# Two-layer hybrid decoder trunk: the up projection as three 256-column matmuls a weight tile, and its activation made for two tiles at once

## Chip, cores and metric

The kernel runs on one core of a Trainium2 chip. The metric is the device time of one execution in microseconds; the number shown is the median of 3 runs.

## What is computed

Two layers over 256 tokens of width 2048, everything in float32. Each layer projects the normed input, mixes it by windowed attention and by gated linear attention, projects back, and ends in a feed-forward part. The change lies in that last part:

```
for l in range(DEPTH):                       # 2 layers
    h = rmsnorm(x, norm1_g[l])
    proj = h @ w_in[l]                       # 2048 -> 4624
...
    x = x + mix @ w_out[l]                   # 2048 -> 2048
    h = rmsnorm(x, norm2_g[l])
    u = jnp.square(jax.nn.relu(h @ w_up[l])) # 2048 -> 8192
    x = x + u @ w_down[l]                    # 8192 -> 2048
```

## The kernel before

All weights stream from HBM once, in blocks of four k-tiles (4 x 128 rows) by up to 512 columns, in a fixed order (`blocks`, made by `plan`). `fetch` issues one DMA a block on SP's queue, four blocks ahead. A float32 product is made from faster fp32r matmuls by splitting both factors into a high and a low part. `prep` splits half a weight block (128 x 1024): ScalarE rounds it to `wh` (L119), VectorE makes `wl` as the rest (L120). Five such halves may lie ahead (`WBUFS`). An activation tile has its 256 high columns (one a token) in columns 0 to 255 and its low ones in 256 to 511. Each product is the sum of high x high, high x low and low x high.

There are two matmul loops. `block_b` (input, output and down projections; tiles `in`, `wo`, `dn`) holds the activations still, and moves `wh`, `wl` and `wh` (L172, L173, L174), 512 columns or 264 where the weight block is that narrow, three matmuls a k-tile into one PSUM sum. `block_a` (up projection, tiles `up`) holds the weights still, because its output shall have the features on the partitions. For each of four 128-column groups f of the block and each of four k-tiles it loads `wh` and moves the whole activation tile, 512 columns (L189), and then loads `wl` and moves the high 256 columns (L191):

```
nc.tensor.matmul(accs[f], wh[:, k % 2, fs], a, ...)            # L189, 512 columns
nc.tensor.matmul(accs[f][:, :S], wl[:, k % 2, fs], a[:, :S])   # L191, 256 columns
```

So a PSUM tile `up` has high x high plus low x high in its left half, and high x low in its right half. Such a pair is called below the work of one weight tile. A chunk of the up projection is 512 features: 4 blocks of 16 weight tiles, 64 pairs. There are 16 chunks a layer, 32 in all, 2048 pairs. The order of chunks is up 0, then (up, up, down) seven times, then up 15 and down 7.

After a chunk, for each f: ScalarE copies the right half to `us` (L779), VectorE adds the left half (L780) and makes relu squared (L781), ScalarE rounds it to the high half of `u` (L783), and VectorE makes the low half (L784). `u` is an activation tile of the down projection, in a pool `uT` of 12 buffers; the attention's and part of the gated attention's output `mx` use the same pool. PSUM has four banks for `up`, `dn`, `in` and `wo`, handed round.

A scheduler of the framework puts the instructions of each engine in order; engines run their own lists in order and wait for each other by semaphores.

Of the kernel before, what the change touches and what calls it, by code (L numbers as in the profile page):

```python
# [8 lines left out]
F32 = mybir.dt.float32  # L9
F32R = mybir.dt.float32r  # L10
BF16 = mybir.dt.bfloat16
U8 = mybir.dt.uint8
AF = mybir.ActivationFunctionType
ALU = mybir.AluOpType
AX = mybir.AxisListType
PSUM = bass.MemoryType.PSUM

P = 128
S = 256
# [16 lines left out]

# Columns of the norm vectors once they lie one element per partition.
C_N2 = 0
# [10 lines left out]
def trunk(ctx, tc, x, norm1_g, w_in, q_norm_g, k_norm_g, attn_sinks, gla_gate_w,  # L49
# [13 lines left out]

# [1 line left out]
    blocks = []  # L65
# [73 lines left out]

    # Work beside the weight stream, handed out between its half blocks ("ticks").  # L140
    side = []
# [18 lines left out]
    def block_b(accs, lhs, first, last, kts):  # L160
        """Tokens on PSUM partitions: accs[T] += act^T W for four k-tiles."""
        i = next_block()
        n = blocks[i][2][1] - blocks[i][2][0]
        hl = (halves.pop(2 * i), halves.pop(2 * i + 1))
        for T in range(NT):
            for k in range(4):
                wh, wl = hl[k // 2]
                a = lhs[kts[k]]
                ah = a[:, T * P:(T + 1) * P]
                al = a[:, S + T * P:S + (T + 1) * P]  # L170
                o = accs[T][:, :n]
                nc.tensor.matmul(o, ah, wh[:, k % 2, :n], start=(first and k == 0), stop=False)  # L172
                nc.tensor.matmul(o, ah, wl[:, k % 2, :n], start=False, stop=False)  # L173
                nc.tensor.matmul(o, al, wh[:, k % 2, :n], start=False,  # L174
                                 stop=(last and k == 3))
            if T or n > 264:
                tick()
        prep_to(2 * i + 2 + WBUFS)

    def block_a(accs, rhs, first, last, kts):  # L180
        """Features on PSUM partitions: accs[f] += W^T act for four k-tiles."""
        i = next_block()
        hl = (halves.pop(2 * i), halves.pop(2 * i + 1))
        for f in range(4):
            for k in range(4):
                wh, wl = hl[k // 2]
                a = rhs[kts[k]]
                fs = slice(f * P, (f + 1) * P)
                nc.tensor.matmul(accs[f], wh[:, k % 2, fs], a,  # L189
                                 start=(first and k == 0), stop=False)  # L190
                nc.tensor.matmul(accs[f][:, :S], wl[:, k % 2, fs], a[:, :S], start=False,  # L191
                                 stop=(last and k == 3))
            if f % 2:
                tick()
        prep_to(2 * i + 2 + WBUFS)

# [1 line left out]
    zeros = const.tile([P, 512], F32, tag="zeros", name="zeros")  # L198
# [46 lines left out]
    def col(c):  # L245
# [6 lines left out]

    # ND[q, j] = -(distance of query q from key j of the two-block band), or far below.
    nd = const.tile([P, 2 * P], F32, tag="nd", name="nd")
# [6 lines left out]
                            base=-1, channel_multiplier=-1)  # L261
    # One where the running sum goes on, zero where a chunk begins.
    goon = const.tile([P, GH * S], BF16, tag="goon", name="goon")
    nc.gpsimd.memset(goon, 1.0)
    nc.gpsimd.memset(goon.rearrange("p (c t) -> p c t", t=CH)[:, :, 0:1], 0.0)
    # caus[s, h, t] = 1 where t >= s.
    causf = const.tile([P, P], F32, tag="causf", name="causf")
# [6 lines left out]

# [1 line left out]
    def power(dst, src, scale):  # L276
        """dst = (src * scale + eps) ** -0.5"""
        nc.gpsimd.tensor_scalar(dst, src, scale, EPS, ALU.mult, ALU.add)
        nc.gpsimd.tensor_tensor(dst, dst, neghalf[:, :dst.shape[-1]], ALU.pow)
# [6 lines left out]
    class Norm:  # L286
        """Sums of squares and the transposed, gained and split x, chunk by chunk."""

# [55 lines left out]
    def head_rs(ps, heads, r, name):  # L344
        """1 / rms per head of z * r, times r; ps holds z."""
        sq = sm.tile([P, 512], F32, tag="junk", name=f"sq{name}")
        nc.scalar.activation(sq[:, :heads * HD], ps, AF.Square, scale=r)
        ss = sm.tile([P, 8], F32, tag="hss", bufs=4, name=f"hss{name}")
        nc.vector.tensor_reduce(ss[:, :heads],
                                sq[:, :heads * HD].rearrange("p (h d) -> p h d", d=HD),  # L350
                                AX.X, ALU.add)
        power(ss[:, :heads], ss[:, :heads], 1.0 / HD)
        nc.gpsimd.tensor_scalar(ss[:, :heads], ss[:, :heads], r, None, ALU.mult)
        return ss[:, :heads]

    def layer(l, norm):
# [10 lines left out]

# [1 line left out]
        kT = at.tile([P, NKV, S], F32, tag="ma", name=f"kT{l}")  # L369
# [60 lines left out]
        def attend(grp):  # L430
# [51 lines left out]
            for T in range(NT):  # L482
                for kb in range(T + 1):
                    for par in range(2):
                        nc.tensor.matmul(  # L485
                            obv[par * HD:(par + 1) * HD, :, T * P:(T + 1) * P],
                            vt[:, kb, grp * HD:(grp + 1) * HD],
                            pT[T, kb][:, par * S:(par + 1) * S].rearrange(
                                "p (a q) -> p a q", q=P),
                            start=(kb == 0), stop=(kb == T))  # L490
            for pr in range(2):
                kt = 2 * grp + pr
                d = act.tile([P, 512], F32R, tag="uT", bufs=12, name=f"mx{l}{kt}")
                src = ob[:, pr * S:(pr + 1) * S]
                nc.scalar.activation(d[:, :S], src, AF.Copy)
                nc.vector.tensor_tensor(d[:, S:], src, d[:, :S].bitcast(F32), ALU.subtract)
                mixT[kt] = d

# [1 line left out]
        # The gate's weights as [H; H; L] against the inputs as [H; L; H].  # L500
        R = 16
# [140 lines left out]
        def scores():  # L642
            """att^T[s, t] of both chunks of a token tile, and of the first with the second."""
            q, kin, kst, dec = g["q"], g["kin"], g["kst"], g["dec"]
            for T in range(NT):
# [13 lines left out]
                nc.vector.copy_predicated(a, caus.rearrange("p h t -> p (h t)"), b)  # L659
                # Decay the first tile's keys to its end, the second tile's queries from  # L660
                # its beginning.
                if T == 0:
# [50 lines left out]
        def finish(silu_steps):  # L713
            yield from silu_steps
            for h in range(GH):
# [7 lines left out]
                for j in range(2):  # L723
                    kt = 2 * h + j
                    for T in range(NT):
                        nc.tensor.transpose(b[:, j * S + T * P:j * S + (T + 1) * P],
                                            on[T][:, kt * P:(kt + 1) * P], ident)
                for j in range(2):
                    kt = 2 * h + j
                    if kt < 4:  # L730
                        d = act.tile([P, 512], F32R, tag="uT", bufs=12, name=f"mx{l}{8 + kt}")
                    else:
                        d = act.tile([P, 512], F32R, tag="hT", bufs=16, name=f"mx{l}{8 + kt}")
                    split_scaled(d, b[:, j * S:(j + 1) * S], col(C_GN + 2 * l + j))
                    mixT[8 + kt] = d
# [6 lines left out]

# [1 line left out]
        evacs = [evac_kv, evac_q(0), evac_q(1), evac_tail, evac_gqk("q"), evac_gqk("k"),  # L744
# [7 lines left out]

# [1 line left out]
        norm2 = Norm(f"f{l}", cols, C_N2 + l * KT, True)  # L754
# [12 lines left out]

# [1 line left out]
        uT = {}  # L769
        hT2 = norm2.hT  # L770
        nxt = Norm(f"i{l + 1}", n1cols, (l + 1) * KT, False) if l + 1 < DEPTH else None
        for kind, i in FFN_ORDER:
            if kind == "up":
                accs = [acc.tile([P, 512], F32, tag="a", name=f"up{l}{i}{f}") for f in range(4)]
                for kb in range(4):
                    block_a(accs, hT2, kb == 0, kb == 3, range(4 * kb, 4 * kb + 4))
                for f in range(4):
                    s = sm.tile([P, S], F32, tag="us", bufs=2, name=f"us{l}{i}{f}")
                    nc.scalar.activation(s, accs[f][:, S:], AF.Copy)  # L779
                    nc.vector.tensor_tensor(s, accs[f][:, :S], s, ALU.add)  # L780
                    nc.vector.scalar_tensor_tensor(s, s, 0.0, s, ALU.max, ALU.mult)  # L781
                    d = act.tile([P, 512], F32R, tag="uT", bufs=12, name=f"u{l}{i}{f}")
                    nc.scalar.activation(d[:, :S], s, AF.Copy)  # L783
                    nc.vector.tensor_tensor(d[:, S:], s, d[:, :S].bitcast(F32), ALU.subtract)  # L784
                    uT[4 * i + f] = d
            else:
# [65 lines left out]
```

## Time and profile before

| | |
|---|---|
| median of 3 runs | 2096.58 us (2096.28 to 2097.39) |
| profiled execution, span from the first to the last instruction | 2094.5 us (its own time with what lies around the span is not recorded; the runs lie 1.8 to 2.9 us above the span) |
| TensorE matmul busy | 2085.8 us, 100% of the span, 10574 matmuls |
| TensorE weight load busy | 1755.6 us, 84% |
| VectorE / ScalarE / GpSimd busy | 61% / 48% / 2% |
| mean granted TensorE clock | 0.999 of full speed |
| DMA | 383.9 MB, mean 183 GB/s, 16 engines about half busy |

How to read it: matmuls are pipelined, so the duration of one (start to modelled end) is longer than the time it takes from the stream. What a matmul costs in a stream is read from the distance between two starts. Weight loads have a row of their own (PEld), beside the matmuls.

### The profile page before, as it was taken

What the parts mean: (1) busy time and instruction counts of PE and PEld (TensorE: products, weight loads), DVE (VectorE), ACT (ScalarE), POOL (GpSimd) and SP (SyncE); (2) the same over time, 40 slices, a digit from 0 to 9 for tenths busy, and PEclk for the clock granted to TensorE, in tenths of its full rate; (3) what the DMA queues carried; (4) which work ended last, traced back from release to release, by engine and by line L of the source; (5) the groups of instructions that cost most, each with busy time, mean ns of one, the idle gap of its engine ahead of it and who ended that gap; (6) DMA issues with size and microseconds to landing.
All of it is one profiled execution on the core that took longest, in us unless ns stands there. A gap on an engine that the chain in (4) does not pass through costs nothing.

```text
span 2094.5 us, 26522 instructions
## 1 busy us (share of the span) xinstructions
PE 2085.8 (100%) x10574; PEld 1755.6 (84%) x10574; DVE 1276.7 (61%) x1678; ACT 1012.4 (48%) x1471; POOL 50.0 (2%) x86
## 2 busy tenths in 40 slices
PE   9999999999999999999999999999999999999999
PEld 7877888888888888888888878888888888888887
DVE  5676665656565565655657766656565665656655
ACT  6565555434444343443555755544444443444433
POOL 3100000000000000000011000000000000000000
PEclk9999999999999999999999999999999999999999
DMA  7544555555565555555555445555555555555554
GB/s 255 181 153 141 162 181 181 188 194 187 175 207 189 187 198 183 198 184 183 192 188 163 159 134 172 184 177 201 181 201 181 201 182 192 190 187 195 187 195 141
DMA packets 197245, 383.93 MB, mean 183 GB/s; under 512 B 6484, under 2 KB 14752, under 8 KB 197120
## 3 DMA queue, kind: packets, MB, share of 16 engines
q1 hardware_dynamic: 195472, 379.87, 54.8%
q10 hardware_dynamic: 1200, 2.11, 0.3%
q8 instruction: 83, 1.36, 0.3%
q0 software_dynamic: 448, 0.24, 0.1%
q14 instruction: 42, 0.34, 0.1%
HBM read 380.10 MB, written 2.10 MB: 182 GB/s over the span
## 4 chain that ended last, share of the span: by engine, by line
PE 99%; DMA 0%; issue 0%; SPq 0%; DVE 0%; ACT 0%
PE up L189 23%; PE up L191 12%; PE dn L174 11%; PE dn L173 11%; PE dn L172 11%; PE in L172 6%; PE in L174 6%; PE in L173 6%; PE wo L172 3%; PE wo L174 3%; PE wo L173 3%; PE sc L440 1%; PE ob L485 1%; PE pt L474 1%; PE hbf L300 0%; PE go L698 0%
## 5 line engine op out<-in xcount | busy, mean ns | idle before, releaser
L120 DVE TENSOR_TENSOR wl<-raw,wh 128x1024 fp32r<-128x1024 f32 (+1 forms) x736 | 872.7, 1200 | 681.5 <-ACT wh L119 664.2
L119 ACT ACTIVATE wh<-raw 128x1024 fp32r<-128x1024 f32 (+1 forms) x736 | 754.3, 1039 | 819.1 <-PE dn L174 352.5
L189 PE MATMUL up<-hf,wh 128*128 128x512 f32 x2048 | 715.1, 397 | 0.0
L191 PE MATMUL up<-hf,wl 128*128 128x256 f32 x2048 | 561.4, 281 | 0.0
L189 PEld LDWEIGHTS up<-hf,wh 128*128 128x128 f32 x2048 | 378.8, 188 | 85.0
L172 PE MATMUL dn<-wh,u 128*128 128x512 f32 x1024 | 399.0, 390 | 0.0
L173 PE MATMUL dn<-wl,u 128*128 128x512 f32 x1024 | 398.6, 389 | 0.0
L174 PE MATMUL dn<-wh,u 128*128 128x512 f32 x1024 | 398.2, 389 | 0.0
L191 PEld LDWEIGHTS up<-hf,wl 128*128 128x128 f32 x2048 | 386.6, 189 | 7.9
L172 PE MATMUL in<-wh,hi 128*128 128x512 f32 (+1 forms) x640 | 239.5, 377 | 3.0 <-ACT hi L282 3.0
L173 PE MATMUL in<-wl,hi 128*128 128x512 f32 (+1 forms) x640 | 236.5, 371 | 0.0
L174 PE MATMUL in<-wh,hi 128*128 128x512 f32 (+1 forms) x640 | 235.2, 371 | 0.0
L172 PEld LDWEIGHTS dn<-wh,u 128*128 128x128 f32 x1024 | 192.2, 188 | 40.1
L174 PEld LDWEIGHTS dn<-wh,u 128*128 128x128 f32 x1024 | 192.2, 188 | 40.0
L173 PEld LDWEIGHTS dn<-wl,u 128*128 128x128 f32 x1024 | 192.2, 188 | 39.4
L172 PEld LDWEIGHTS in<-wh,hi 128*128 128x128 f32 x640 | 119.9, 188 | 25.2 <-ACT hi L282 3.3
L174 PEld LDWEIGHTS in<-wh,hi 128*128 128x128 f32 x640 | 120.2, 188 | 21.1 <-issue 0.8
L173 PEld LDWEIGHTS in<-wl,hi 128*128 128x128 f32 x640 | 120.3, 188 | 19.9 <-issue 0.4
L795 DVE SCALAR_TENSOR_TENSOR x<-dn,vf,x 128x512 f32<-128x512 f32 x128 | 95.6, 748 | 35.8 <-PE dn L174 35.8
L173 PE MATMUL wo<-wl,mx 128*128 128x512 f32 x256 | 100.7, 393 | 0.0
L174 PE MATMUL wo<-wh,mx 128*128 128x512 f32 x256 | 99.9, 392 | 0.0
L172 PE MATMUL wo<-wh,mx 128*128 128x512 f32 x256 | 99.5, 396 | 0.0
(165 smaller groups left out, 1051.8 us busy)
## 6 DMA issues: line engine op xcount, KB each, us to landing
raw<-in_w_up_dram SPq DMA_DIRECT2D x128, 1024.0 KB, 5.1
raw<-in_w_down_dram SPq DMA_DIRECT2D x128, 1024.0 KB, 5.0
raw<-in_w_in_dram SPq DMA_DIRECT2D x63, 1024.0 KB, 5.1
raw<-in_w_out_dram SPq DMA_DIRECT2D x32, 1024.0 KB, 5.0
raw<-in_w_in_dram SPq DMA_DIRECT2D x16, 528.0 KB, 3.7
x<-in_x_dram SPq DMA_DIRECT2D x8, 256.0 KB, 9.6
out_dram<-x ACTq DMA_DIRECT2D x8, 256.0 KB, 2.8
raw<-in_w_in_dram SPq DMA_DIRECT2D x2, 512.0 KB, 7.1
```

The source lines that it names most:

```text
L119: nc.scalar.activation(wh[:, :, :n], src, AF.Copy)
L120: nc.vector.tensor_tensor(wl[:, :, :n], src, wh[:, :, :n].bitcast(F32), ALU.subtract)
L172: nc.tensor.matmul(o, ah, wh[:, k % 2, :n], start=(first and k == 0), stop=False)
L173: nc.tensor.matmul(o, ah, wl[:, k % 2, :n], start=False, stop=False)
L174: nc.tensor.matmul(o, al, wh[:, k % 2, :n], start=False, stop=(last and k == 3))
L189: nc.tensor.matmul(accs[f], wh[:, k % 2, fs], a, start=(first and k == 0), stop=False)
L191: nc.tensor.matmul(accs[f][:, :S], wl[:, k % 2, fs], a[:, :S], start=False, stop=(last and k == 3))
L440: nc.tensor.matmul(sb[par][:, j * nk:(j + 1) * nk], qT[par * HD:(par + 1) * HD, 2 * (grp % 2) + j, T * P:(T + 1) * P], kT[par * HD:(par + ...
L474: nc.tensor.transpose(b[:, j * P:(j + 1) * P], t[:, h, kb * P:(kb + 1) * P], ident)
L485: nc.tensor.matmul(obv[par * HD:(par + 1) * HD, :, T * P:(T + 1) * P], vt[:, kb, grp * HD:(grp + 1) * HD], pT[T, kb][:, par * S:(par + 1) ...
L795: nc.vector.scalar_tensor_tensor(xs[T, n], accs[T], norm2.r[:, T:T + 1], xs[T, n], ALU.mult, ALU.add)
```

## The change

`block_a` makes three matmuls of 256 columns for a weight tile: `wh` against the high activations, `wl` against the high ones, `wh` against the low ones, all into the left half of the PSUM tile. The third one needs `wh` in the array again, after `wl`. The right half of the bank is no longer written. After a chunk there is nothing left to add: ScalarE copies two such sums beside each other into a `us` tile of 512 columns, and relu squared, the high half and the low half of `u` are made for both tiles by one instruction each. `u` tiles are allocated in pairs (6 buffers of 2 x 512 in place of 12 of 512), and so are the `mx` tiles that use the pool. Comments are removed, which moves no instruction.

```diff
     def block_a(accs, rhs, first, last, kts):
...
         for f in range(4):
+            o = accs[f][:, :S]
             for k in range(4):
...
-                nc.tensor.matmul(accs[f], wh[:, k % 2, fs], a,
+                nc.tensor.matmul(o, wh[:, k % 2, fs], a[:, :S],
                                  start=(first and k == 0), stop=False)
-                nc.tensor.matmul(accs[f][:, :S], wl[:, k % 2, fs], a[:, :S], start=False,
+                nc.tensor.matmul(o, wl[:, k % 2, fs], a[:, :S], start=False, stop=False)
+                nc.tensor.matmul(o, wh[:, k % 2, fs], a[:, S:], start=False,
                                  stop=(last and k == 3))
...
-                for f in range(4):
-                    s = sm.tile([P, S], F32, tag="us", bufs=2, name=f"us{l}{i}{f}")
-                    nc.scalar.activation(s, accs[f][:, S:], AF.Copy)
-                    nc.vector.tensor_tensor(s, accs[f][:, :S], s, ALU.add)
+                for f in range(2):
+                    s = sm.tile([P, 512], F32, tag="us", bufs=2, name=f"us{l}{i}{f}")
+                    for j in range(2):
+                        nc.scalar.activation(s[:, j * S:(j + 1) * S], accs[2 * f + j][:, :S],
+                                             AF.Copy)
                     nc.vector.scalar_tensor_tensor(s, s, 0.0, s, ALU.max, ALU.mult)
-                    d = act.tile([P, 512], F32R, tag="uT", bufs=12, name=f"u{l}{i}{f}")
-                    nc.scalar.activation(d[:, :S], s, AF.Copy)
-                    nc.vector.tensor_tensor(d[:, S:], s, d[:, :S].bitcast(F32), ALU.subtract)
-                    uT[4 * i + f] = d
+                    d = act.tile([P, 2, 512], F32R, tag="uT", bufs=6, name=f"u{l}{i}{f}")
+                    s2 = s.rearrange("p (f t) -> p f t", t=S)
+                    nc.scalar.activation(d[:, :, :S], s2, AF.Copy)
+                    nc.vector.tensor_tensor(d[:, :, S:], s2, d[:, :, :S].bitcast(F32),
+                                            ALU.subtract)
+                    for j in range(2):
+                        uT[4 * i + 2 * f + j] = d[:, j]
```

The order on TensorE at the start of the first chunk of the up projection (`up` is the PSUM sum, `hf` an activation tile; each matmul brings a weight load of its own, which isn't listed). Before:

```order
L189 MATMUL up_3029<-hf_2631,wh_0_2954 128x512
L191 MATMUL up_3029<-hf_2631,wl_0_2955 128x256
L189 MATMUL up_3029<-hf_2634,wh_0_2954 128x512
L191 MATMUL up_3029<-hf_2634,wl_0_2955 128x256
L189 MATMUL up_3029<-hf_2664,wh_1_2984 128x512
L191 MATMUL up_3029<-hf_2664,wl_1_2985 128x256
```

Now:

```order
L190 MATMUL up_3023<-hf_2625,wh_0_2948 128x256
L192 MATMUL up_3023<-hf_2625,wl_0_2949 128x256
L193 MATMUL up_3023<-hf_2625,wh_0_2948 128x256
L190 MATMUL up_3023<-hf_2628,wh_0_2948 128x256
L192 MATMUL up_3023<-hf_2628,wl_0_2949 128x256
L193 MATMUL up_3023<-hf_2628,wh_0_2948 128x256
```

Where one matmul of 512 columns and one of 256 stood, three of 256 stand; no two neighbours share their weights.

The order on ScalarE at the end of that first chunk (`us` from `up` is the copy out of PSUM, `u` the rounding, `wh` the split of a coming weight half). Before:

```order
L779 ACTIVATE us_3232<-up_3029 128x256
L779 ACTIVATE us_3239<-up_3030 128x256
L783 ACTIVATE u_3236<-us_3232 128x256
L783 ACTIVATE u_3243<-us_3239 128x256
L119 ACTIVATE wh_1_3224<-raw_3086 128x1024
L779 ACTIVATE us_3246<-up_3031 128x256
L119 ACTIVATE wh_0_3228<-raw_3143 128x1024
L779 ACTIVATE us_3253<-up_3032 128x256
L783 ACTIVATE u_3250<-us_3246 128x256
L783 ACTIVATE u_3257<-us_3253 128x256
L119 ACTIVATE wh_1_3298<-raw_3143 128x1024
```

Now:

```order
L785 ACTIVATE us_3290<-up_3023 128x256
L785 ACTIVATE us_3290<-up_3024 128x256
L790 ACTIVATE u_3294<-us_3290 128x2x256
L785 ACTIVATE us_3297<-up_3025 128x256
L119 ACTIVATE wh_1_3282<-raw_3096 128x1024
L119 ACTIVATE wh_0_3286<-raw_3169 128x1024
L785 ACTIVATE us_3297<-up_3026 128x256
L790 ACTIVATE u_3301<-us_3297 128x2x256
L119 ACTIVATE wh_1_3358<-raw_3169 128x1024
```

Two roundings became one, the third copy moved ahead of a weight split, and the fourth copy stands behind two splits. SP's and GpSimd's lists keep their order.

## Rows read from the trace of the kernel before

**Rows 1.** The page's head, and its first part: busy time and share by engine.
```profile
span 2094.5 us, 26522 instructions
PE 2085.8 (100%) x10574; PEld 1755.6 (84%) x10574; DVE 1276.7 (61%) x1678; ACT 1012.4 (48%) x1471; POOL 50.0 (2%) x86
```

**Rows 2.** The page's groups on TensorE: count | busy us, mean ns | idle before, releaser.
```profile
L189 PE MATMUL up<-hf,wh 128*128 128x512 f32 x2048 | 715.1, 397 | 0.0
L191 PE MATMUL up<-hf,wl 128*128 128x256 f32 x2048 | 561.4, 281 | 0.0
```

**Rows 3.** Timeline of PE, two up chunks (128 pairs): first row, row behind the last.
```profile
453.19 0.39 PE L189 MATMUL up<-hf,wh 128*128 128x512 f32 x1
...
498.17 0.39 PE L172 MATMUL dn<-wh,u 128*128 128x512 f32 x1
```

**Rows 4.** Windows: length, PE busy, PEld busy, DVE, ACT, POOL, granted clock, DMA.
```profile
453.20:498.10 44.90, 44.90 (x257) 39.09 (x256) 25.95 (x35) 19.95 (x28) 0.00 (x0) 1.00 0.54 183
...
238.00:249.40 11.40, 11.40 (x97) 11.40 (x96) 11.40 (x16) 6.27 (x10) 0.00 (x0) 1.00 0.62 200
```

**Rows 5.** Timeline of PE, a down chunk: first and last of 24 matmuls.
```profile
699.77 0.39 PE L172 MATMUL dn<-wh,u 128*128 128x512 f32 x1
...
704.99 0.39 PE L174 MATMUL dn<-wh,u 128*128 128x512 f32 x1
```

**Rows 6.** Timeline of PE, a 264-column chunk of 96: first row, row behind the last.
```profile
237.97 0.28 PE L172 MATMUL in<-wh,hi 128*128 128x264 f32 x1
...
249.50 0.62 PE L172 MATMUL wo<-wh,mx 128*128 128x512 f32 x2
```

**Rows 7.** Timeline of PE, another 264-column chunk: first and last of 31 matmuls.
```profile
92.31 0.28 PE L174 MATMUL in<-wh,hi 128*128 128x264 f32 x1
...
95.95 0.28 PE L174 MATMUL in<-wh,hi 128*128 128x264 f32 x1
```

**Rows 8.** Timeline of PE, three pairs of another up chunk.
```profile
900.00 0.28 PE L191 MATMUL up<-hf,wl 128*128 128x256 f32 x1
900.12 0.40 PE L189 MATMUL up<-hf,wh 128*128 128x512 f32 x1
900.36 0.28 PE L191 MATMUL up<-hf,wl 128*128 128x256 f32 x1
900.47 0.40 PE L189 MATMUL up<-hf,wh 128*128 128x512 f32 x1
900.71 0.28 PE L191 MATMUL up<-hf,wl 128*128 128x256 f32 x1
900.82 0.40 PE L189 MATMUL up<-hf,wh 128*128 128x512 f32 x1
```

**Rows 9.** Groups on DVE and ACT, shapes apart: count | busy us, mean ns | idle before, releaser.
```profile
L780 DVE TENSOR_TENSOR us<-up,us 128x256 f32<-128x256 f32 x128 | 53.7, 419 | 6.8 <-ACT us L779 6.8
L784 DVE TENSOR_TENSOR u<-us,u 128x256 fp32r<-128x256 f32 x128 | 50.1, 422 | 9.6 <-ACT u L783 2.4
L781 DVE SCALAR_TENSOR_TENSOR us<-us 128x256 f32<-128x256 f32 x128 | 48.0, 417 | 0.0
L765 DVE TENSOR_TENSOR x<-wo,x 128x512 f32<-128x512 f32 x16 | 11.0, 688 | 4.8 <-PE wo L174 4.8
L795 DVE SCALAR_TENSOR_TENSOR x<-dn,vf,x 128x512 f32<-128x512 f32 x128 | 95.6, 748 | 35.8 <-PE dn L174 35.8
L634 ACT ACTIVATE gv<-in,ri 128x512 f32<-128x512 f32 x8 | 5.4, 680 | 4.3 <-PE in L174 3.3 <-PE sc L440 1.0
```

**Rows 10.** Waits, longest first: who waited for whom: us in total, times, longest.
```profile
ACT wh L119 <- PE dn L174: 352.5, 214, 3.0
ACT wh L119 <- PE up L189: 291.1, 96, 4.8
```

**Rows 11.** Timelines of ACT, DVE and PE where down 7 follows up 15 at once.
```profile
2047.27 1.05 ACT L119 ACTIVATE wh<-raw 128x1024 fp32r<-128x1024 f32 x1
2048.22 0.37 ACT L779 ACTIVATE us<-up 128x256 f32<-128x256 f32 x1
...
2053.15 0.42 DVE L784 TENSOR_TENSOR u<-us,u 128x256 fp32r<-128x256 f32 x1
...
2052.07 0.39 PE L172 MATMUL dn<-wh,u 128*128 128x512 f32 x1
```

More of the change, by code (lines that the diff above doesn't have):

```diff
@@ L490, in attend @@
                             start=(kb == 0), stop=(kb == T))
+            d2 = act.tile([P, 2, 512], F32R, tag="uT", bufs=6, name=f"mx{l}{grp}")
             for pr in range(2):
                 kt = 2 * grp + pr
-                d = act.tile([P, 512], F32R, tag="uT", bufs=12, name=f"mx{l}{kt}")
+                d = d2[:, pr]
                 src = ob[:, pr * S:(pr + 1) * S]
@@ L727, in finish @@
                                             on[T][:, kt * P:(kt + 1) * P], ident)
+                if h < 2:
+                    d2 = act.tile([P, 2, 512], F32R, tag="uT", bufs=6, name=f"mxg{l}{h}")
                 for j in range(2):
@@ L730, in finish @@
                     if kt < 4:
-                        d = act.tile([P, 512], F32R, tag="uT", bufs=12, name=f"mx{l}{8 + kt}")
+                        d = d2[:, j]
                     else:
```

## The prediction

> **What bounds the kernel now.** I read the busy shares first [rows 1]. The reader should see that TensorE's matmul row is full (2085.8 of 2094.5 us), with VectorE at 61% and ScalarE at 48%. Then the groups on TensorE [rows 2]: the idle time before both lines of the up projection is 0.0, over 2048 instructions each. So no matmul of the up projection waits for weights, for an activation or for a free PSUM bank, and what counts is how fast TensorE runs through its own list. A busy row of pipelined matmuls doesn't say that (the means, 397 and 281 ns, overlap), so I went to the timeline and measured from start to start.
>
> Two chunks of the up projection in a row take 498.17 - 453.19 = 44.98 us for 128 pairs [rows 3], **351.4 ns a pair** of a 512-column and a 256-column matmul. Times 2048 pairs that is 719.7 us, a third of the span. In that stretch the clock was granted in full (1.00, 2.4 GHz) and the weight loads cover 39.09 of 44.90 us [rows 4].
>
> **What the change adds on TensorE.** For each weight tile one matmul of 512 columns and one of 256 go, three of 256 come. The columns moved stay at 768; there is one matmul and one weight load more, 2048 of each in all. Nothing waits on anything else, so the whole term is 2048 x (3 g - 351.4 ns), where g is the start-to-start time of a 256-column fp32r matmul in a stream of its like. The point of no change is g = 117.1 ns. The trace of before has no such stream, so g is bounded by neighbours.
>
> - A stream of 512: 23 steps from 699.77 to 704.99, 227.0 ns each [rows 5]. 512 columns at 2.4 GHz are 213.3 ns, so a matmul costs 13.7 ns beyond its columns. The same added to 256 columns (106.7 ns) gives g = 120.4.
> - A stream of 264, three matmuls a k-tile into one PSUM sum, just the new pattern but for 8 columns: 96 steps from 237.97 to 249.50, 120.1 ns each [rows 6]. Another such stretch: 30 steps from 92.31 to 95.95, 121.3 ns [rows 7]. Here the weight-load row is full: 11.40 of 11.40 us [rows 4]. Taken as it is, this bounds g from above, at 121.3.
> - The 256-column slots inside the present pairs: 900.00 to 900.12, 900.36 to 900.47, 900.71 to 900.82, mean 113 ns [rows 8]. Each is followed by a 512-column slot of 240 ns or so (900.12 to 900.36, 900.47 to 900.71), which is 13 ns longer than in the stream of 512. What the short slot gains the long one pays, so 113 is a lower bound, and an unlikely one.
> - Straight line through the streams of 264 and 512: (227.0 - 120.1) / 248 = 0.431 ns a column, so 8 columns fewer make g = 116.7.
>
> I take **g = 120.0**. The nearest row is the 264-column stream, and it says 120.1. Whether to take 3.3 ns off for its 8 extra columns is the choice that decides the sign. I don't, for two reasons: the fixed cost in the stream of 512 leads to 120.4 by another way, and in the 264 stream the loads are packed without a gap, so it is as likely that loading 128 weight columns sets the pace there as the columns moved, and a load is the same for 256. Then a weight tile costs 360.0 in place of 351.4 ns, +8.6 ns, and the term is 2048 x 8.6 = **+17.6 us**. The ends: 113 gives 3 x 113 - 351.4 = -12.4 ns, -25.4 us; 121.3 gives +12.5 ns, +25.6 us.
>
> There is a rule to hold against this. In the present pairs a 512 and a 256 take 351.4 ns, 31.4 ns above their 768 columns [rows 3]. The Trainium skill ("TensorE: Matmul & The Clock Gate", section "Back-to-back issue gap") gives the gap between warm matmuls as columns / 2.4 GHz plus about 2.5 ns. By it, as an estimate, a third matmul would cost only one more 2.5 ns, and the sum would be 2048 x 2.5 = +5.1 us. The rows here don't bear the size out: the overhead is 13.7 ns a matmul in the stream of 512 and about 10 in that of 264.
>
> **What it takes from VectorE and ScalarE.** Before, VectorE spends 419 + 422 + 417 ns a tile, 161.0 us over 128 tiles [rows 9]. After, a pair of tiles takes one product of 512 columns and one difference of 512; priced by the 512-column forms of the same operations, 748 and 688 ns [rows 9], that is 64 x 1.436 = 91.9 us, some 69 us less. ScalarE keeps 128 copies of 256 columns; 128 roundings of 417 ns at most become 64 of 680 [rows 9], some 10 us less. I cost all of it at nothing: TensorE was not waiting for them (idle 0.0 [rows 2]), and ScalarE itself waits 291.1 and 352.5 us for TensorE to free weight buffers [rows 10]. If that cover were gone, up to 69 us would count; nothing in the rows suggests it.
>
> **Moved waits.** The rounding of two tiles now waits for the later of them, and the fourth copy stands behind two weight splits. Behind the rounding on ScalarE queues the next split, which works five halves ahead and waits for buffers anyway [rows 10]. Who needs `u` soon? Only down 7, which follows up 15 at once, twice in the kernel. Before, its first matmul on the new chunk starts at 2052.07, and the last `u` is done at 2053.15 + 0.42 = 2053.57, in time for the fourth k-tile (2052.07 + 9 x 0.227 = 2054.1) [rows 11, 5]. After: the last copy again about 2048.6, a weight difference ahead of it on VectorE to about 2049.8, then 0.75 + 0.68 + 0.69, done about 2051.9. That is ahead of the need. Cost 0; at worst a microsecond or so in each layer.
>
> A PSUM bank is read once by ScalarE instead of by ScalarE and then VectorE, so it comes free sooner; no one waited, so no gain. DMA, the blocks and SP's queue stay the same.
>
> **Sum:** 2094.5 + 17.6 = 2112.1 us of span. The runs lie about 2.1 us above the span (2096.58 against 2094.5), so 2114.2, or **2114**, a change of +0.84%. A measurement of this kernel tells about 0.2% (4.2 us) from no change; that is 2.0 ns a weight tile, g between 116.4 and 117.8.
>
> **Rivals.**
>
> *The columns set the pace, and the fixed part is small* (the straight line). g = 116.7, 350.1 ns a weight tile, -1.3 ns, -2.7 us: about 2094, no change. For it: the 264 stream has only 10 ns beyond its columns, so overhead isn't the same everywhere. Against it: that stream's load row is full. Chance 0.20. The rule of the Trainium skill above ("TensorE: Matmul & The Clock Gate", "Back-to-back issue gap") is of this kind, with its +5.1 us; the trace agrees with it in kind at most, not in the size of the fixed part.
>
> *Mixing is what costs, and equal matmuls run better* (the other side). The pair costs 351.4, while the streams would give 227.0 + 117 to 120 = 344 to 347 for it; so 4 to 7 ns a pair are lost where long and short alternate, and the short slot alone shows 113. If a uniform stream of 256 keeps 113, a weight tile takes 339 ns, -25.4 us: 2071. It decides for faster from g below 116.4. Against it: the 264 stream is uniform and shows 120. Chance 0.12.
>
> *The short stream falls into the uneven rhythm of rows 7.* g = 121.3, +25.6 us: 2122. The stretches of 264 show both; which one a stream gets, I can't tell from the trace. Chance 0.15.
>
> *The change doesn't do what it says:* the third matmul could save its load if `wh` were still in the array. The order lists `wl` between, and before, each matmul has a load (10574 of each [rows 1]). I give it nothing of its own.
>
> *`u` comes late at every chunk.* Down reads chunks that are a whole up chunk old, but for the two places above. With other small stalls: 0.02, slower.
>
> **How the numbers follow.** Forecast (g = 120) 0.51, uneven rhythm 0.15, stalls 0.02: slower 0.68. Straight line: same 0.20. Uniform gain: faster 0.12. The range takes in the straight line and the uneven rhythm, with about 2 us at each end: 2092 to 2125; it leaves out the gain, and a little at the top.
>
> **What the profile of the changed kernel would show.** TensorE still 100% busy with idle 0.0 on all three lines of the up projection; 12622 matmuls and as many loads; start to start 120 ns there, 360 a weight tile; load row full in those stretches; two up chunks in a row 46.1 us in place of 44.98. VectorE near 1208 us. The down and input projections unchanged at 227 ns. I'd be wrong if the starts stand below 117 ns apart, or if idle time shows up ahead of `dn` or `up`.

## The result, and the profile after

The changed kernel takes 2113.58 us (median of 4 runs, 2113.25 to 2114.2), the kernel before 2096.84 us beside it. The ratio is 1.0079, with a 95% interval of 1.0067 to 1.0091: slower by 0.8%. The forecast was 2114, with a range of 2092 to 2125.

The page of the changed kernel, head and busy shares, answers to [rows 1]:

```profile
span 2111.6 us, 30040 instructions
PE 2103.2 (100%) x12622; PEld 1866.2 (88%) x12622; DVE 1228.2 (58%) x1422; ACT 1005.4 (48%) x1407; POOL 48.5 (2%) x86
```

The span grew by 2111.6 - 2094.5 = 17.1 us and TensorE's busy time by 17.4. TensorE was full and is full. There are 2048 matmuls and 2048 loads more, as many loads as matmuls again. VectorE and ScalarE do less, and it shows nowhere in the end.

The page's groups on TensorE (count | busy us, mean ns | idle before), for [rows 2]:

```profile
L190 PE MATMUL up<-hf,wh 128*128 128x256 f32 x2048 | 579.8, 283 | 0.0
L193 PE MATMUL up<-hf,wh 128*128 128x256 f32 x2048 | 579.6, 283 | 0.0
L192 PE MATMUL up<-hf,wl 128*128 128x256 f32 x2048 | 579.6, 283 | 0.0
```

No line of the up projection waits. The timeline of PE over two up chunks in a row, first row and the row behind the last, answers to [rows 3]:

```profile
454.47 0.28 PE L190 MATMUL up<-hf,wh 128*128 128x256 f32 x1
...
500.54 0.40 PE L172 MATMUL dn<-wh,u 128*128 128x512 f32 x1
```

500.54 - 454.47 = 46.07 us for 384 matmuls: **120.0 ns each, 359.9 ns a weight tile**, in place of 351.4. Times 2048 weight tiles the difference of 8.5 ns is 17.4 us: the whole result.

The window over the same stretch (length, PE, PEld, DVE, ACT, POOL, clock, DMA) answers to [rows 4]:

```profile
454.50:500.50 46.00, 46.00 (x385) 46.00 (x384) 23.52 (x23) 19.83 (x26) 0.00 (x0) 1.00 0.57 182
```

The weight-load row is now full from end to end, as in the stretch of 264 columns before. That looks like a load that sets the pace. The experiments show that it isn't so.

The groups of the activation, by shape:

```profile
L791 DVE TENSOR_TENSOR u<-us,u 128x512 fp32r<-128x512 f32 x64 | 44.3, 693 | 44.7 <-ACT u L790 44.7
L787 DVE SCALAR_TENSOR_TENSOR us<-us 128x512 f32<-128x512 f32 x64 | 44.1, 688 | 17.9 <-ACT us L785 17.9
L785 ACT ACTIVATE us<-up 128x256 f32<-128x256 f32 x128 | 47.9, 375 | 38.6 <-PE up L193 38.4
L790 ACT ACTIVATE u<-us 128x512 fp32r<-128x512 f32 x64 | 40.5, 633 | 82.2 <-DVE us L787 82.2
```

And the waits of the weight split for TensorE, for [rows 10]:

```profile
ACT wh L119 <- PE dn L174: 355.3, 229, 3.0
ACT wh L119 <- PE up L193: 311.8, 96, 4.0
```

ScalarE waits a little longer for TensorE than before (352.5 and 291.1 us in [rows 10]). The time that it was given back lengthened its wait.

### The profile page after: what moved, and what is told of

Its sections match the earlier page's. It is cut to its first block, busy times and chain, and to the rows that moved or that the text cites. A ratio compares the mean times of both kernels' runs of the same rounds, so it can differ in the third digit from the quotient of the medians.

```text
span 2111.6 us, 30040 instructions
## 1 busy us (share of the span) xinstructions
PE 2103.2 (100%) x12622; PEld 1866.2 (88%) x12622; DVE 1228.2 (58%) x1422; ACT 1005.4 (48%) x1407; POOL 48.5 (2%) x86
## 4 chain that ended last, share of the span: by engine, by line
PE 99%; DMA 0%; issue 0%; SPq 0%; DVE 0%; ACT 0%
PE up L193 12%; PE up L192 12%; PE up L190 12%; PE dn L173 11%; PE dn L172 11%; PE dn L174 11%; PE in L172 6%; PE in L174 6%; PE in L173 6%; PE wo L172 3%; PE wo L174 3%; PE wo L173 3%; PE sc L442 1%; PE ob L487 1%; PE pt L476 0%; PE hbf L302 0%
## 5 line engine op out<-in xcount | busy, mean ns | idle before, releaser
L190 PE MATMUL up<-hf,wh 128*128 128x256 f32 x2048 | 579.8, 283 | 0.0
L193 PE MATMUL up<-hf,wh 128*128 128x256 f32 x2048 | 579.6, 283 | 0.0
L192 PE MATMUL up<-hf,wl 128*128 128x256 f32 x2048 | 579.6, 283 | 0.0
L190 PEld LDWEIGHTS up<-hf,wh 128*128 128x128 f32 x2048 | 393.1, 192 | 0.6
L192 PEld LDWEIGHTS up<-hf,wl 128*128 128x128 f32 x2048 | 393.1, 192 | 0.6
L193 PEld LDWEIGHTS up<-hf,wh 128*128 128x128 f32 x2048 | 393.1, 192 | 0.0
L790 ACT ACTIVATE u<-us 128x512 fp32r<-128x512 f32 x64 | 40.5, 633 | 82.2 <-DVE us L787 82.2
```

The lines of the kernel that those rows point to most:

```text
L190: nc.tensor.matmul(o, wh[:, k % 2, fs], a[:, :S], start=(first and k == 0), stop=False)
L192: nc.tensor.matmul(o, wl[:, k % 2, fs], a[:, :S], start=False, stop=False)
L193: nc.tensor.matmul(o, wh[:, k % 2, fs], a[:, S:], start=False, stop=(last and k == 3))
L790: nc.scalar.activation(d[:, :, :S], s2, AF.Copy)
```

## The experiments

Two questions were open behind a forecast that came out: does the activation's part really count for nothing, and why does a 256-column matmul take 120 ns? Theory 1 says the load of 128 weight columns sets that pace, theory 2 that it is the columns moved plus a fixed part. The medians of the kernel before lay at 2096.8 to 2097.4 us beside these runs.

### The activation alone, undone and done

The pairing undone in the changed kernel:

```diff
...
-                    nc.vector.scalar_tensor_tensor(s, s, 0.0, s, ALU.max, ALU.mult)
...
+                        s = sm.tile([P, S], F32, tag="us", bufs=2, name=f"us{l}{i}{f}")
+                        nc.scalar.activation(s, accs[f][:, :S], AF.Copy)
+                        nc.vector.scalar_tensor_tensor(s, s, 0.0, s, ALU.max, ALU.mult)
...
```

Here the rounding and the difference behind it are made tile by tile too.

> The three 256-column matmuls of the change, but u made tile by tile again (the pairing undone; no addition). Theory (TensorE's stream alone sets the time): as the change, 2113.6 us within 3, ratio 1.008 to before, 360 ns a weight tile. Rival (the pairing of u gives time back that the third matmul costs): slower than the change, by up to the 40 to 60 us that VectorE and ScalarE do more.

Measured: 2113.57 us (2112.06 to 2116.3), ratio to before 1.0081, 1.0066 to 1.0096. The theory's number.

```profile
PE 2102.9 (100%) x12622; PEld 1865.8 (88%) x12622; DVE 1238.4 (59%) x1550; ACT 1015.5 (48%) x1471; POOL 50.0 (2%) x86
```

The matmuls of before, with the pairing (the addition now goes into each half of a 512-column tile):

```diff
+                    s = sm.tile([P, 512], F32, tag="us", bufs=2, name=f"us{l}{i}{f}")
...
+                        sj = s[:, j * S:(j + 1) * S]
+                        nc.scalar.activation(sj, accs[2 * f + j][:, S:], AF.Copy)
+                        nc.vector.tensor_tensor(sj, accs[2 * f + j][:, :S], sj, ALU.add)
                     nc.vector.scalar_tensor_tensor(s, s, 0.0, s, ALU.max, ALU.mult)
...
```

> The matmuls of before (512 and 256), the addition kept, but relu squared and both halves of u made for two tiles at once. Theory (VectorE and ScalarE are hidden): 2096.8 us within 3, ratio 1.000. Rival (they are partly on the path): faster, by up to some 30 us.

Measured: 2095.74 us (2094.98 to 2098.32), ratio 0.9994, 0.9985 to 1.0004: no difference that can be told from noise. So of the two parts of the change, the matmuls carry all of the time and the activation none, within what can be measured.

### Long and short matmuls in streams of their own

The second rival said that alternating 512 and 256 columns costs something. Runs of four for each f, in the kernel before:

```diff
             for k in range(4):
...
                 nc.tensor.matmul(accs[f], wh[:, k % 2, fs], a,
                                  start=(first and k == 0), stop=False)
+            for k in range(4):
...
                 nc.tensor.matmul(accs[f][:, :S], wl[:, k % 2, fs], a[:, :S], start=False,
                                  stop=(last and k == 3))
```

> Before, but for each f first the four 512-column matmuls, then the four of 256. Theory (alternating long and short costs 4 ns a pair; in streams of their own they take 227 and 120 ns): (4 x 227 + 4 x 120) / 4 = 347 ns in place of 351.4, 2048 x -4.4 = -9 us, 2087.8 us, ratio 0.9957. Rival (the changeover from long to short costs the same wherever it stands, or the short one gains by the long neighbour): 2096.8 or, if each short one takes 124, slower by 0 to 8 us.

Measured: 2095.66 us (2093.85 to 2097.13), ratio 0.9994, 0.9984 to 1.0003: a miss for the theory's 2087.8, and near the rival's 2096.8. The timeline of PE over the same two chunks, first row, a place inside, and the row behind the last. It merges neighbours of one line, and the count stands at the end:

```profile
455.94 1.07 PE L189 MATMUL up<-hf,wh 128*128 128x512 f32 x4
...
460.12 1.09 PE L189 MATMUL up<-hf,wh 128*128 128x512 f32 x4
461.05 0.28 PE L195 MATMUL up<-hf,wl 128*128 128x256 f32 x1
461.17 1.08 PE L189 MATMUL up<-hf,wh 128*128 128x512 f32 x4
462.09 0.98 PE L195 MATMUL up<-hf,wl 128*128 128x256 f32 x7
...
500.74 0.40 PE L172 MATMUL dn<-wh,u 128*128 128x512 f32 x1
```

The scheduler moved some matmuls (the 1 and the 7 here), but the width changes as often as the source has it: counted through the two chunks, 63 times, against 245 times in the kernel before, where the scheduler had already put some equal widths together. The two chunks take 500.74 - 455.94 = 44.80 us, 350.0 ns a weight tile. That is 1.4 ns less than before, an estimated 3 us in all, too little to be told from noise in the medians. Four of 512 here take 461.05 - 460.12 = 0.93 us, 232 ns each and not 227.

Longer runs:

```diff
...
+        if last:
+            for f in range(4):
+                high(f)
+                low(f)
...
+        else:
+            for part in (high, low):
+                for f in range(4):
+                    part(f)
```

Here `high(f)` makes the four 512-column matmuls of f and `low(f)` the four of 256.

> Before, but in the first three blocks of a chunk sixteen 512-column matmuls, then sixteen of 256; in the last block runs of four. Theory: the same 347 ns a weight tile as with runs of four, 2087.8 us within 2. Rival (each changeover of the width has its price): faster than runs of four, since three quarters of the blocks have a quarter of the changeovers.

Measured: 2092.36 us (2090.89 to 2093.35), ratio **0.9976, 0.9967 to 0.9986**. Faster than both kernels, by half of what was expected. The timeline, two chunks from first row to the row behind the last, and places inside them:

```profile
454.04 1.98 PE L186 MATMUL up<-hf,wh 128*128 128x512 f32 x8
455.85 0.52 PE L191 MATMUL up<-hf,wl 128*128 128x256 f32 x3
456.21 1.09 PE L186 MATMUL up<-hf,wh 128*128 128x512 f32 x4
457.14 1.23 PE L191 MATMUL up<-hf,wl 128*128 128x256 f32 x9
...
463.26 2.08 PE L191 MATMUL up<-hf,wl 128*128 128x256 f32 x16
465.17 3.82 PE L186 MATMUL up<-hf,wh 128*128 128x512 f32 x16
...
498.73 0.40 PE L172 MATMUL dn<-wh,u 128*128 128x512 f32 x1
```

Sixteen stand together only at some places. The source has 27 changes of width in two chunks, the timeline 39. 44.69 us for 128 weight tiles are 349.1 ns each, 2.3 ns less than before, 4.6 us in all; the medians differ by 4.8. Sixteen short ones take 465.17 - 463.26 = 1.91 us, 119.4 ns each, also here, among long ones.

A pair from settled streams would take 227.0 + 120.0 = 347.0 ns. Above that lie 4.4 ns before with 245 changes, 3.0 with 63, and 2.1 with 39. So mixing does cost, and fewer changes cost less. But a change has no fixed price: spread over the changes the loss is 2.3 ns each before, and 6 to 7 in these two kernels. Nor is their number all: in the run with the pairing alone 247 changes take 44.88 us, where the kernel before has 245 in 44.98. The theory was wrong in taking runs of four for settled streams; the last rival, that each change of width has its price, holds in kind.

Both together (these runs and the pairing with the addition):

> Before with both: sixteen 512-column matmuls, then sixteen of 256, in the first three blocks of a chunk, runs of four in the last; and relu squared and both halves of u made for two tiles at once (the addition kept). Theory (only TensorE's stream counts): as with the runs of sixteen alone, 2092.4 us within 2, ratio 0.998 to before, 0.990 to the change. Rival (the pairing gives time of its own): under 2090.

Measured: 2093.59 us (2091.67 to 2094.69), ratio 0.9980, 0.9971 to 0.9989, the same as without the pairing. The best version is this order (written as runs of sixteen), with either form of the activation.

### What the 120 ns are made of

These runs, one execution timed of each, change the shape of the change's matmuls (the last one only their order). In the runs with fewer columns all but the first k-tile and the last of a chunk are cut, 5376 of 6144 matmuls; with 288 columns all are changed.

```diff
...
+                c = S if (first and k == 0) or (last and k == 3) else 192
+                o = accs[f][:, :c]
-                nc.tensor.matmul(o, wh[:, k % 2, fs], a[:, :S],
+                nc.tensor.matmul(o, wh[:, k % 2, fs], a[:, :c],
...
```

> The change, with only 192 tokens' columns moved in all but the first and the last k-tile of a chunk (15 of 16 k-tiles in four, that is 14 of 16: 5376 of 6144 matmuls; the last 64 tokens miss those terms). Theory 1 (the load sets the pace): still 120 ns, 2113.6. Theory 2 (columns plus a fixed 13.3 ns): 80 + 13.3 = 93.3 ns, 5376 x -26.7 = -143 us, 1970. Third: fewer columns than 256 are moved slower a column, over 120 ns.

Measured: 2067.74 us. That is neither theory 1 (2113.6) nor theory 2 (1970).

With 288 columns:

```diff
-            o = accs[f][:, :S]
+            o = accs[f][:, :288]
...
-                nc.tensor.matmul(o, wl[:, k % 2, fs], a[:, :S], start=False, stop=False)
-                nc.tensor.matmul(o, wh[:, k % 2, fs], a[:, S:], start=False,
+                nc.tensor.matmul(o, wl[:, k % 2, fs], a[:, :288], start=False, stop=False)
+                nc.tensor.matmul(o, wh[:, k % 2, fs], a[:, 224:], start=False,
...
```

> The change, with 288 columns moved by each of the three matmuls in place of 256 (32 columns of the other half ride along, and the low ones come in shifted, so the sums aren't those of the reference). Theory 1 (loading the 128 weight columns sets the pace of 120 ns): 288 columns are 120 ns of moving themselves, so 120 to 124 ns start to start, at most +25 us: 2114 to 2138. Theory 2 (columns plus a fixed 13.3 ns): 133.3 ns, 6144 x 13.3 = +82 us, 2195.

Measured: 2190.58 us, near theory 2's 2195. The span grew by 2188.8 - 2111.6 = 77.2 us, 12.6 ns for each of 6144 matmuls, nearly the 13.3 ns of 32 columns at 2.4 GHz. That speaks against theory 1: if the load of 128 set the pace at 256, the first columns added would have been free. One row fits badly: the 264-column stream takes 120.1 [rows 6], so there 8 more columns than 256 cost nothing. The run with 192 columns decides, as its timeline below shows.

With half of the weight columns:

```diff
...
+                c = P if (first and k == 0) or (last and k == 3) else 64
+                fs = slice(f * P, f * P + c)
+                o = accs[f][:c, :S]
...
```

> The change, with 256 columns moved but only 64 of the 128 weight columns loaded in 5376 of 6144 matmuls (the other 64 features of each tile miss those terms). Theory 1 (the load sets the pace): the load halves, the columns come to the front: 107 to 113 ns, 5376 x -7 to -13 = -38 to -70 us, 2044 to 2076. Theory 2 (columns plus a fixed part): 120 ns, 2113.6; if the fixed part goes with the weights loaded, 113.3.

Measured: 2081.6 us, above theory 1's 2044 to 2076 and far below theory 2's 2113.6. It is near theory 2's other case, a fixed part that goes with the weights: 113.3 ns, 2113.6 - 5376 x 6.7 ns = 2078.

The timelines of PE in these three kernels, in the order told, first and last row of a stretch of equal matmuls:

```profile
455.26 0.27 PE L193 MATMUL up<-hf,wl 128*128 128x192 f32 x1
...
456.71 0.27 PE L194 MATMUL up<-hf,wh 128*128 128x192 f32 x1
```

```profile
467.85 0.29 PE L190 MATMUL up<-hf,wh 128*128 128x288 f32 x1
...
471.95 0.29 PE L192 MATMUL up<-hf,wl 128*128 128x288 f32 x1
```

```profile
469.83 0.28 PE L194 MATMUL up<-hf,wh 128*64 128x256 f32 x1
...
471.08 0.28 PE L193 MATMUL up<-hf,wl 128*64 128x256 f32 x1
```

13 steps of 111.5 ns with 192 columns; 31 steps of 132.3 ns with 288; 11 steps of 113.6 ns with 256 columns and 64 weight columns (113.8 on average over all such steps of the trace). With 192 columns the same load of 128 is done every 111.5 ns, so it isn't what holds the change at 120.0: theory 1 falls. From these I formed a third theory: columns moved plus a quarter of the columns loaded, and beneath it a floor of 111 ns that a load of 128 takes by itself. Three more runs test it.

With 224 columns moved (the edit as for 192):

> The change with 224 columns moved and 128 weight columns loaded in 5376 of 6144 matmuls (the last 32 tokens miss those terms). Theory 3: by columns 93.3 + 13.3 = 106.7 ns, so the load's own 111 ns sets the pace, as with 192: 5376 x -9 = -48 us, 2065. Rival (no floor; 192 was slow because it is short): 106.7 ns, -71 us, 2042.

With 64 weight columns and 192 moved:

> The change with both cuts at once in 5376 of 6144 matmuls: 192 columns moved, 64 weight columns loaded (those terms are missing elsewhere). Theory 3: 80 + 6.7 = 86.7 ns, as the load of 64 is far under 111 by itself: 5376 x -33.3 = -179 us, 1935, if weights still arrive in time (a block then lasts 4.2 us). Rival (the 111 ns seen with 192 columns are a floor of narrow matmuls, not of the load): 111 ns, 2066.

With 32 weight columns (the edit as for 64):

> The change, 256 columns moved, only 32 of the 128 weight columns loaded in 5376 of 6144 matmuls (96 features of each tile miss those terms). Theory 3, formed on the runs with 64 weight columns (113) and with 288 moved (132): a matmul takes its moved columns plus a quarter of the loaded weight columns, both at 2.4 GHz, as long as that is over some 111 ns that a load of 128 takes by itself: 106.7 + 3.3 = 110 ns, 5376 x -10 = -54 us, 2060. Rival (a fixed part of 13.3 ns of which half went with the load): 106.7 + 6.7, no further gain, 113 ns, 2081.

Measured: 2067.62, 1951.39 and 2087.36 us. The timelines, in that order, the last kernel at two places:

```profile
455.11 0.28 PE L193 MATMUL up<-hf,wl 128*128 128x224 f32 x1
...
456.67 0.28 PE L191 MATMUL up<-hf,wh 128*128 128x224 f32 x1
```

```profile
454.76 0.25 PE L195 MATMUL up<-hf,wh 128*64 128x192 f32 x1
...
455.82 0.25 PE L195 MATMUL up<-hf,wh 128*64 128x192 f32 x1
```

```profile
470.03 0.28 PE L193 MATMUL up<-hf,wl 128*32 128x256 f32 x1
...
470.82 0.28 PE L194 MATMUL up<-hf,wh 128*32 128x256 f32 x1
```

```profile
367.05 0.28 PE L191 MATMUL up<-hf,wh 128*32 128x256 f32 x1
...
380.36 0.28 PE L194 MATMUL up<-hf,wh 128*32 128x256 f32 x1
```

With 224 columns, 14 steps of 111.4 ns: the same as with 192, so there is a floor. With 192 columns and 64 weight columns, 12 steps of 88.3 ns: the floor is gone with half of the load, so it belongs to the load and not to narrow matmuls. Both speak for theory 3, the second with 2 ns more than its 86.7 and 16 us more than its 1935.

With 32 weight columns there are two rhythms: 7 steps of 112.9 ns at the first place, 113 steps of 117.8 at the second, 115.6 on average over all such steps. So there is no gain over 64 (the run is 5.8 us slower), where theory 3 had 110 and 2060. That part of it falls. Its rival, a fixed part of which half went with the load (113, 2081), fits the better of the two rhythms; where the other comes from, no run here shows. By these averages the fixed part is 7 to 9 ns with 32 or 64 weight columns, and some 13 with 128.

The same weights next to each other:

```diff
                 nc.tensor.matmul(o, wh[:, k % 2, fs], a[:, :S],
                                  start=(first and k == 0), stop=False)
-                nc.tensor.matmul(o, wl[:, k % 2, fs], a[:, :S], start=False, stop=False)
-                nc.tensor.matmul(o, wh[:, k % 2, fs], a[:, S:], start=False,
+                nc.tensor.matmul(o, wh[:, k % 2, fs], a[:, S:], start=False, stop=False)
+                nc.tensor.matmul(o, wl[:, k % 2, fs], a[:, :S], start=False,
                                  stop=(last and k == 3))
```

> The change, with the two matmuls on the same high weights next to each other (high x high, low x high, then high x low). Theory (each matmul loads its weights whether they are there or not): 12622 loads, 120 ns, 2113.6. Rival (a repeated load is left out or is shorter): fewer loads; where the load sets the pace the weight tile takes 347 ns or less, 2087 or less.

Measured: 2113.43 us, with as many loads as before:

```profile
PE 2103.4 (100%) x12622; PEld 1866.2 (88%) x12622; DVE 1226.9 (58%) x1422; ACT 1005.4 (48%) x1407; POOL 49.8 (2%) x86
```

A repeated load is made again. Whether the third matmul could go without one, given an instruction stream without it, was not tried.

## Why the prediction was right, point by point

**TensorE's stream alone sets the time.** Right. Idle time 0.0 before all three lines, and the two halves of the change, run apart, gave 1.0081 and 0.9994.

**g = 120.0 ns, +17.6 us.** Right: 120.0 and +17.4. Of the two reasons for not taking 3.3 ns off the 264-column stream, the first holds. A matmul of 128 weight columns costs some 13 ns beyond its columns at 256 (120.0 - 106.7 = 13.3) and 288 (132.3 - 120.0 = 12.3) as at 512 (227.0 - 213.3 = 13.7). With it the term can be read in two parts: splitting the long matmul adds one fixed part, 3 x 120.0 - 347.0 = 13.0 ns, and the 4.4 ns that mixing had cost come back, which leaves the measured 8.5 but for rounding.

The second reason, that the load is as likely to set the pace at 256, is wrong. With 128 weight columns the pace doesn't fall below 111 ns; that is close, and a stream of 224 columns meets it (111.4). The full load row of [rows 4] misled: it is full at 256 columns, where the columns decide, and full too in a stretch of the run with 64 weight columns, where the steps are 113 ns and half as much is loaded (12.50 of 12.50 us):

```profile
371.00:383.50 12.50, 12.50 (x113) 12.50 (x112) 5.13 (x6) 5.18 (x6) 0.00 (x0) 1.00 0.64 215
```

The straight line (no change) is rejected by the 120.0 itself. Its slope came from the 264-column stream at 120.1 [rows 6], which is some 3 ns faster than 110 + 13.3 would be. Why that stream is faster than the rule, no run here shows. So that its 120.1, taken as it is, gave g to 0.1 ns is in part luck: what 8 columns more should cost is as large as what this stream saves. The way by the stream of 512 (120.4) is the one that the runs bear out.

By the gap formula of the Trainium skill ("TensorE: Matmul & The Clock Gate", section "Back-to-back issue gap") the third matmul would have cost 2.5 ns a weight tile, +5.1 us as an estimate. The section calls that formula the gap of an isolated matmul, and says that in a stream with weight loads both set the spacing. The trace disagrees with its size for these fp32r streams with their loads: 8.5 ns, +17.4 us.

**The uniform stream that keeps 113.** It did not come: a uniform stream takes 120. The 113 was a misreading. Three steps, printed to 10 ns, were too few [rows 8]: over the whole trace of the kernel before the short slots take 116.9 ns on average and the long ones 234.4, so the short slot gains 3 ns and the long one pays 7, in place of 7 and 13. The prediction was right that the long slot pays for the short one, and the rival's other half was true too: mixing does cost, and with fewer changes of width the kernel before becomes 0.24% faster.

**The uneven rhythm (121.3).** It did not come: 384 matmuls in 46.07 us leave no room for it.

**`u` in time for down 7.** Right. The timelines of DVE and PE in the changed kernel, at the last such place, answer to [rows 11]:

```profile
2067.71 0.69 DVE L791 TENSOR_TENSOR u<-us,u 128x512 fp32r<-128x512 f32 x1 [0.70 <-ACT u L790]
```

```profile
2068.94 0.39 PE L172 MATMUL dn<-wh,u 128*128 128x512 f32 x1
```

The last `u` is done at 2068.40, ahead of the first matmul on the new chunk at 2068.94.

**VectorE near 1208 us.** Off by 20: it is 1228.2, so 48.5 us less than before, not 69. The working multiplied mean durations, and neighbours overlap in the records. By the groups' busy time before was 53.7 + 50.1 + 48.0 = 151.8 [rows 9] and after 44.3 + 44.1 = 88.4, still 63 less. The groups overlap each other and the other lines too: worked out from the trace, the three lines before added 133 us to the row, and the two after add 86. Nothing hung on it.

## What to carry to other kernels

On a full TensorE, price a change of shapes from start to start in a settled stream, and not from mean durations or from the busy share of the load row. Splitting a 512-column fp32r matmul into two of 256 costs one fixed part more (some 13 ns with 128 weight columns here), and below an estimated 235 columns ((111.4 - 13.3) x 2.4) the floor of 111 ns takes over. Relief for engines that wait for TensorE was worth nothing here (0.9994), and a source order is only what the scheduler leaves of it: read the order back, and count in it what the experiment is about, before reading a result from it.

## What was not expected of the hardware

The fixed part of a matmul fell with the weight columns loaded, but not in proportion: 13.3 ns with 128, and 7 to 9 with 64 and with 32. Changing width within a stream costs too: a weight tile takes 351.4 ns in alternation, 350.0 in runs of four and 349.1 in the longer runs, while settled streams of 227.0 and 120.0 would give 347.0. What happens inside TensorE at a change of width stays open.
